# A macaron layer in split fp32: sums spread over the second product's blocks, the passages between its stages rearranged

## The chip, the core and the metric

The kernel runs on one core of a Trainium2 chip. The metric is device time in microseconds of one execution; the kernel before has a median of 1325.62 us over three runs. In the profile PE is TensorE's matmuls, PEld its weight loads, DVE VectorE, ACT ScalarE, POOL GpSimd and SP the engine whose queue issues nearly all the transfers.

## The reference

One layer, 512 tokens of width 1024, all in float32: a feed-forward half step, a token mixer with two branches (a chunked matrix LSTM and an attention with forgetting), and a second feed-forward half step, each with an RMS norm whose gain and shift come from a conditioning vector c.

```python
def swiglu(u, w_in, w_out):
    a, b = jnp.split(u @ w_in, 2, axis=-1)
    return (jax.nn.silu(a) * b) @ w_out

mod = jax.nn.silu(c) @ w_ada + b_ada
sh1, sc1, g1, sh2, sc2, g2, sh3, sc3, g3 = ...
u = rms_norm(x, ffn1_norm_g) * (1 + sc1) + sh1
x = x + 0.5 * g1 * swiglu(u, ffn1_w_in, ffn1_w_out)
u = rms_norm(x, mix_norm_g) * (1 + sc2) + sh2
z = u @ w_mix + b_mix
...
x = x + g2 * (merged @ w_out)
u = rms_norm(x, ffn2_norm_g) * (1 + sc3) + sh3
x = x + 0.5 * g3 * swiglu(u, ffn2_w_in, ffn2_w_out)
```

The hidden width is 2816 (22 blocks of 128), w_mix has some 8200 columns.

## The kernel before

**Split products.** Each float32 product is made of three matmuls on a rounded high half and the rest: hi x hi, lo x hi, hi x lo (mm3, lines 127 to 129; in the passage after FFN1 lines 1397 to 1400). A weight block of 128 x 1024 numbers is loaded into one of three buffers (`raw`, line 92, the loads are issued by SP in order), ScalarE rounds it to the high half (wh, line 102), VectorE subtracts for the low half (wl, line 104); wh and wl have four buffers each. A load may start when the wl that used its buffer three loads earlier is done.

**Activations.** Tokens lie on partitions for x (tiles x[tb][half], four token blocks by two halves of 512 columns) and on the free axis for u = norm(x), which is the transposed xn times G plus sh: ScalarE writes the rounded uh, a second operation the unrounded uf, a third ul = uf - uh. A norm works on two token blocks at once, "half 0" and "half 1", 256 columns of u each: squares on ScalarE as each x tile is finished (x_sq, line 229), a chain of nine small VectorE operations (lines 146 to 154 and 247), four xn, 16 transposes on TensorE (line 295), eight uh, uf and ul.

**Output product of a feed-forward (pair_out, line 515).** The hidden blocks are paired, 11 pairs (NP), and the 512 tokens too, after a Strassen-like scheme: a first product gives sums P1, U2, U4 (two tiles each), the second one works on eight banks X, W, Z, Y, each for two token blocks. Pair i needs a block c of w_out and a block d of precomputed sums of weights (`ws`, in DRAM). i = 0 to 7 run pair by pair; the last three (tail) are closed bank by bank, their d blocks loaded ahead (`early`, we). P1, U2 and U4 are scaled by 0.5 g (line 597) and added to x (line 600) at i = 6 and 7 in the program; where no order is pinned, a scheduler places them. x itself is loaded at i = 3 to 6 into tiles that the first product has used.

**Passages.** After FFN1, `end` closes the banks in a written order (keep_in_program_order, `pin`), adds Z and Y to the first half of the tokens, makes the norm of half 0 while X and W close, and runs the first four column blocks m = 0 to 3 of w_mix on half 0, then on half 1. GpSimd makes every second ul of half 0. After the mixer, token_gemm (half 1 of w_out's columns) makes the last x tiles; norm_half is called for half 0 ahead of the last token block's matmuls and for half 1 behind it, with ul of odd k on GpSimd (line 267) and uf on VectorE (line 266); ffn_in_halves then does the first two hidden blocks of FFN2 by halves. Rows of w_ada for the conditioning vector are worked off in between (acc, line 325).

Of the kernel before, what the change touches and what calls it, by code (L numbers as in the profile page):

```python
# [11 lines left out]
F32 = mybir.dt.float32  # L12
# [8 lines left out]
P = 128  # L21
# [26 lines left out]
class Layer:  # L48
# [209 lines left out]
    def u_from(self, ps, k, c0, w, G, sh, pool):  # L258

        nc = self.nc  # L260
        uf = self.tmp(pool, "uf")
        nc.scalar.activation(self.uh[k][:, c0:c0 + w], ps, AF.Identity, scale=G, bias=sh)
        if self.uf_act:
            nc.scalar.activation(uf[:, :w], ps, AF.Identity, scale=G, bias=sh)
        else:
            nc.vector.tensor_scalar(uf[:, :w], ps, G, sh, op0=MUL, op1=ADD)
        (nc.gpsimd if k % 2 else nc.vector).tensor_tensor(  # L267
            self.ul[k][:, c0:c0 + w], uf[:, :w], self.uh[k][:, c0:c0 + w], op=SUB)

# [12 lines left out]
    def norm_half(self, hf, pool, G, sh):  # L282

        xn = self.xnorm(hf, pool)
        self.norm_u(hf, self.norm_turn(hf, xn), pool, G, sh)

# [11 lines left out]

    def norm_u(self, hf, b, pool, G, sh):
        for k in range(NK):  # L300
            self.u_from(b[k // 2][:, k % 2 * 256:(k % 2 + 1) * 256], k, hf * 256, 256, G[:, k:k + 1], sh[:, k:k + 1], pool)
# [109 lines left out]

    def ffn_in_halves(self, w_in, nj, hp, tp):

        wa = [self.w_stat(w_in, j * P) for j in range(nj)]
        wb = [self.w_stat(w_in, FF + j * P) for j in range(nj)]
        pp = [(self.gbank(), self.gbank()) for _ in range(nj)]
        for h in range(2):
            for j in range(nj):
                c0, c1 = h * 256, (h + 1) * 256
                self.gemm_stat(pp[j][0], wa[j], c0, c1)  # L420
                self.gemm_stat(pp[j][1], wb[j], c0, c1)
                self.pair_h(self.pair_s(pp[j][0], c0, c1, tp), pp[j][1], j, c0, c1, hp, tp)


# [102 lines left out]
    def pair_out(self, w, v, hp, tp, x_src, end=None):  # L527
# [52 lines left out]
        banks = {"Z": Z, "Y": Y, "X": X, "W": W}  # L580
        def prepare(i, d=None):
            c = two(both(2 * i + 1))
            d = d or two(self.ws[i][:, 1:3, :])
# [4 lines left out]
        step = lambda n, tb, i, o: mm(banks[n], tb, *o[n], i == 0, i == NP - 1)  # L588
# [19 lines left out]
        tail, ds = 3, []  # L608
        for i in range(NP - tail):
# [27 lines left out]

        for n in "XZYW":
            for tb in range(2):
                ps = close(n, tb)  # L640
# [9 lines left out]
    def token_gemm(self, lhs, nk, w, half, done, tail=2, extra=None, last=None):  # L650
# [18 lines left out]
        for tb in range(NT):  # L669
            if last and tb == NT - 1:  # L670
                last()
# [4 lines left out]
    def residual(self, factor, v, half, tp, final=False):  # L676
# [3 lines left out]
        def done(tb, half, ps):  # L680
            s = slice(half * 512, (half + 1) * 512)
            t = self.tmp(tp, "rs")
            nc.vector.scalar_tensor_tensor(t, ps, factor, g, op0=MUL, op1=MUL)
            x = self.x[tb][half]
            nc.vector.tensor_tensor(x, x, t, op=ADD)
            if not final:
                self.x_sq(tb, half, t)
            else:
                nc.sync.dma_start(self.out[0, tb * P:(tb + 1) * P, s], x)
# [899 lines left out]
```

## Time and profile before

| | |
|---|---|
| median of three runs | 1325.62 us (1324.99 to 1326.6) |
| profiled execution | 1324.8 us, its span 1323.0 us, granted clock 0.999 |
| busy | PE 1304.9, PEld 1091.7, DVE 958.1, ACT 624.2, POOL 43.7 us |
| chain that ended last | PE 89%, DVE 4%, DMA 3%, ACT 2%, issue 1% |
| FFN1's second product, after which the first passage ends it | about 313 to 376 us of the span |
| second passage | about 955 to 985 us |
| last matmul ends, span ends | 1318.2, 1323.0 us |

A row of the timeline gives start, duration, engine, line of the kernel, operation, output<-inputs, shape, how many of them, and in brackets the idle time before it with what ended it. A row of the windows gives length, then busy time of PE, PEld, DVE, ACT and POOL, PE's granted clock, the share of DMA and GB/s. A row of the waits gives who waited for whom, microseconds in total, times, longest.

### The profile page before, as it was taken

Reading aid. Unit: us, or ns where it says so; the run is one execution under the profiler, and the core shown is the slowest. Engines: PE = TensorE matmul, PEld = TensorE weight load, DVE = VectorE, ACT = ScalarE, POOL = GpSimd, SP = SyncE. Lnnn points to the kernel's source line nnn. Section 1 sums busy time; section 2 is a strip of 40 time slices with the busy share of each in tenths; the row PEclk is TensorE's granted clock in tenths of the full one; section 3 lists DMA queues with packets and bytes.
Section 4 is the critical chain, followed back from the end, with each engine's and each line's share of the span. In section 5 each row is a group of like instructions: output and inputs, shape, how many; then the busy total and the mean of one; then the engine's idle time right before and its main releaser. Section 6 shows DMA issues by size and latency. Waiting matters only on the chain.

```text
span 1323.0 us, 17767 instructions
## 1 busy us (share of the span) xinstructions
PE 1304.9 (99%) x6332; PEld 1091.7 (83%) x6332; DVE 958.1 (72%) x1740; ACT 624.2 (47%) x1038; POOL 43.7 (3%) x65
## 2 busy tenths in 40 slices
PE   7999999999999999999999999999999999999998
PEld 6788888888799888888888788878888888888886
DVE  6877777477788687887877778777577656635777
ACT  5633233355476555566566666334262223223742
POOL 1000000000010101000000000003010000000000
PEclk9999999999999999999999999999999999999999
DMA  9999978465845434533243536777439777624574
GB/s 289 272 327 306 309 251 298 133 195 170 293 118 145 120 104 133 151 104 117 83 120 88 159 98 205 225 245 227 162 97 332 273 233 276 208 96 142 169 260 153
DMA packets 204344, 254.18 MB, mean 192 GB/s; under 512 B 14992, under 2 KB 146480, under 8 KB 204256
## 3 DMA queue, kind: packets, MB, share of 16 engines
q1 hardware_dynamic: 203872, 252.98, 60.0%
q8 instruction: 50, 0.82, 0.3%
q14 instruction: 38, 0.31, 0.1%
q0 software_dynamic: 320, 0.06, 0.0%
q10 hardware_dynamic: 64, 0.02, 0.0%
HBM read 217.28 MB, written 35.72 MB: 191 GB/s over the span
## 4 chain that ended last, share of the span: by engine, by line
PE 89%; DVE 4%; DMA 3%; ACT 2%; issue 1%; SPq 0%; POOL 0%; DVEq 0%; ACTq 0%; POOLq 0%
PE g L129 23%; PE g L127 23%; PE g L128 23%; PE t L128 4%; PE t L129 4%; PE t L127 4%; PE g L825 2%; PE t L1208 1%; PE t L1178 1%; DVE wl L104 1%; DMA x<-x_d 1%; PE t L1149 1%; PE t L825 1%; DMA raw<-in_ffn_w_out_dram 1%; PE t L1150 1%
## 5 line engine op out<-in xcount | busy, mean ns | idle before, releaser
L102 ACT ACTIVATE wh<-raw 128x1024 fp32r<-128x1024 f32 (+2 forms) x250 | 254.2, 1019 | 380.6 <-DMA raw<-in_ffn_w_in_dram 106.4
L104 DVE TENSOR_TENSOR wl<-raw,wh 128x1024 fp32r<-128x1024 f32 (+2 forms) x250 | 293.0, 1174 | 179.3 <-ACT wh L102 155.5
L128 PE MATMUL g<-ul,wh 128*128 128x512 f32 (+1 forms) x912 | 348.1, 383 | 1.1 <-POOL ul L267 1.1
L127 PE MATMUL g<-uh,wh 128*128 128x512 f32 (+1 forms) x912 | 348.7, 384 | 0.0
L129 PE MATMUL g<-uh,wl 128*128 128x512 f32 (+1 forms) x912 | 348.3, 382 | 0.0
L128 PEld LDWEIGHTS g<-ul,wh 128*128 128x128 f32 x912 | 171.3, 188 | 34.5 <-POOL ul L267 1.9
L129 PEld LDWEIGHTS g<-uh,wl 128*128 128x128 f32 x912 | 171.5, 188 | 33.6
L127 PEld LDWEIGHTS g<-uh,wh 128*128 128x128 f32 x912 | 171.0, 188 | 32.5 <-issue 0.6
L325 DVE SCALAR_TENSOR_TENSOR acc<-raw,ccol,acc 128x512 f32<-128x512 f32 (+1 forms) x70 | 66.8, 975 | 43.6 <-DMA raw<-in_w_ada_dram 43.5
L127 PE MATMUL g<-wh,uh 128*128 128x512 f32 (+1 forms) x256 | 97.4, 381 | 0.0
L129 PE MATMUL g<-wh,ul 128*128 128x512 f32 (+1 forms) x256 | 96.6, 378 | 0.0
L128 PE MATMUL g<-wl,uh 128*128 128x512 f32 (+1 forms) x256 | 96.4, 377 | 0.0
L128 PE MATMUL t<-wl,A 128*128 128x512 f32 x176 | 69.0, 392 | 1.7 <-DVE wl L104 1.7
L127 PE MATMUL t<-wh,A 128*128 128x512 f32 x176 | 68.6, 390 | 0.0
L129 PEld LDWEIGHTS g<-wh,ul 128*128 128x128 f32 x256 | 48.1, 188 | 9.0
L127 PEld LDWEIGHTS g<-wh,uh 128*128 128x128 f32 x256 | 48.2, 188 | 8.7 <-DVE tk L1046 0.5
L128 PEld LDWEIGHTS g<-wl,uh 128*128 128x128 f32 x256 | 48.2, 188 | 8.3
L129 PE MATMUL g<-yh,wl 128*128 128x512 f32 x128 | 50.1, 392 | 0.3 <-DVE wl L104 0.3
L127 PE MATMUL g<-yh,wh 128*128 128x512 f32 x128 | 49.8, 389 | 0.0
L128 PE MATMUL g<-yl,wh 128*128 128x512 f32 x128 | 49.8, 389 | 0.0
L455 ACT ACTIVATE A<-E 128x768 fp32r<-128x768 f32 x22 | 18.6, 846 | 57.0 <-DVE E L454 51.1
L1160 ACT ACTIVATE S<-S,mn 128x128 f32<-128x128 f32 (+1 forms) x64 | 35.6, 558 | 16.0 <-DVE mn L1152 9.9
(343 smaller groups left out, 2185.2 us busy)
## 6 DMA issues: line engine op xcount, KB each, us to landing
raw<-in_ffn_w_in_dram SPq DMA_DIRECT2D x82, 512.0 KB, 5.1
raw<-in_w_ada_dram SPq DMA_DIRECT2D x56, 512.0 KB, 5.5
raw<-in_w_mix_dram SPq DMA_DIRECT2D x46, 512.0 KB, 4.5
sa<-in_ffn_w_out_dram SPq DMA_DIRECT2D x22, 512.0 KB, 5.9
sb<-in_ffn_w_out_dram SPq DMA_DIRECT2D x44, 256.0 KB, 5.9
ws<-sa SPq DMA_DIRECT2D x22, 512.0 KB, 3.9
ws<-sb SPq DMA_DIRECT2D x44, 256.0 KB, 4.2
raw<-ws SPq DMA_DIRECT2D x44, 256.0 KB, 3.5
```

The lines of the kernel that those rows point to most:

```text
L102: nc.scalar.activation(hi, src, AF.Copy)
L104: self.last_lo = nc.vector.tensor_tensor(lo, src, hi, op=SUB)
L127: pin(mm(ps, lh, rh, start=start, stop=False))
L128: pin(mm(ps, lh, rl, start=False, stop=False))
L129: self.last_mm = pin(mm(ps, ll, rh, start=False, stop=stop))
L325: nc.vector.scalar_tensor_tensor(a, r[:, s], c, a, op0=MUL, op1=ADD)
L455: nc.scalar.activation(A1[:, 0:3, :], E[:, 0:3, :], AF.Copy)
L825: pin(nc.tensor.matmul(acc_ps[b], (wl if p == 1 else wh)[:, b % 2, s], self.ul[k] if p == 2 else self.uh[k], start=k == 0 and p == 0, stop ...
L1149: nc.tensor.matmul(ps[:, :w], q[:, s], k[:, :w], start=True, stop=False)
L1150: nc.tensor.matmul(ps[:, :w], q[:, s], kl[:, :w], start=False, stop=True)
L1160: nc.scalar.activation(S[:, ws], S[:, ws], AF.Exp, scale=-1.0, bias=m, accum_out=sm[:, qb:qb + 1])
L1178: tr = lambda b, c, qb, kb: nc.tensor.transpose(b[:, c:c + P], S[:, P_OFF[qb] + kb * P:P_OFF[qb] + (kb + 1) * P], self.ident)
```

## The change

**pair_out, both feed-forwards.** The d block of odd i up to 7 is loaded into a fourth buffer of its own (`two_x`, a tile with the tag "xn", the space of a tile that the first half of pair_out has used) and not into the ring. P1, U2 and U4 are scaled in place at i = 0, 1 and 2, and added to x at i = 4 to 7, one token block each time. Their number stays: six scalings, eight sums.

**End of FFN2.** Bank W[1]'s accumulation is closed after i = 7 and its sum added early; the last three pairs of it go into two banks of 256 columns, each scaled, added and stored by itself.

**First passage.** ScalarE copies the X banks to SBUF (`keep`); `other` scales the copy for one half, `both` adds the W bank to the copy, and one scaling of this sum serves where two were. The high halves of m = 2, 3 are placed behind the copies.

**Second passage.** token_gemm's second half, the norm and FFN2's first blocks are written out in one pinned order (`passage`): the transposes of half 0 come after the first three matmuls of the last token block, uf is all ScalarE's and ul all VectorE's, the first four weight blocks of FFN2's w_in run on half 0 (m = 0, 1, then 2, the transposes of half 1, then 3) and then on half 1; the pairs' silu and product come behind, 512 columns at a time.

```diff
+        def two_x(src):
+            t = tp.tile(sh, F32, name=self.nm("raw"), tag="xn", bufs=1)
+            nc.sync.dma_start(t, src)
+            return self.split(t, sh)
...
-            d = d or two(self.ws[i][:, 1:3, :])
+            d = d or (two_x if i % 2 else two)(self.ws[i][:, 1:3, :])
...
-            if i in (6, 7):
-                tb = i - 6
-                add(P1[tb], 0, (tb,))
-                add(U2[tb], 0, (tb + 2,))
-                add(U4[tb], 1, (tb, tb + 2))
+            for src, half in ((P1, 0), (U2, 0), (U4, 1))[i:i + 1]:
+                for tb in range(2):
+                    scaled(src[tb], half, src[tb])
+            if i >= 4:
+                tb = i - 4
+                onto(tb, 0, (P1, U2)[tb // 2][tb % 2])
+                onto(tb, 1, U4[tb % 2])
...
+        add(W[1], 0, (3,))
         for n in "XZYW":
             for tb in range(2):
+                if n == "W" and tb:
+                    for c in (slice(0, 256), slice(256, 512)):
+                        ps, x, r = self.gbank((P, 256)), self.x[3][0][:, c], slice(P, 2 * P)
...
+                        t = self.tmp(tp, "rs")[:, :256]
+                        nc.vector.scalar_tensor_tensor(t, ps, 0.5, g[0][:, c], op0=MUL, op1=MUL)
+                        V(x, x, t, op=ADD)
+                        nc.sync.dma_start(self.out[0, 3 * P:4 * P, c], x)
+                    continue
...
                     X = [close("X", tb) for tb in range(2)]
                     W = [close("W", 0)]
+                    xs = [keep(tb, 0) for tb in range(2)]
+                    pin(nc.scalar.activation(xs[0], X[0], AF.Copy))
+                    hi2()
                     xn = self.xnorm(0, tp)
                     b = self.norm_turn(0, xn)
                     W.append(close("W", 1))
-                    tx = {}
-                    for tb in range(2):
-                        for h in (1, 0):
...
-                            tx[tb, h] = scaled(X[tb], h, t)
+                    pin(nc.scalar.activation(xs[1], X[1], AF.Copy))
+                    hi3()
+                    x1 = {}
+                    def other(tb):
+                        x1[tb] = scaled(xs[tb], 1, keep(tb, 1))
+                    def both(tb):
+                        pin(V(xs[tb], W[tb], xs[tb], op=ADD))
+                    other(0)
+                    both(0)
+                    scaled(xs[0], 0, xs[0])
+                    other(1)
...
-                    w0 = scaled(W[0], 0)
+                    both(1)
                     lo1(4, NK)
```

The second passage's core:

```diff
+        xn = self.xnorm(0, bp)
+        step(3, 1, wcs[0], (0,))
+        b = self.norm_turn(0, xn)
+        step(3, 1, wcs[0], (1,))
+        step(3, 2, wcs[1])
+        step(3, 3, wcs[2])
...
+        first(0, (0, 1))
+        hi3()
+        lo3()
+        first(0, (2,))
+        b = self.norm_turn(1, xn)
+        first(0, (3,))
+        for k in range(NK):
+            part(1, b, k, True)
+        first(1, (0, 1))
+        first(1, (2,))
+        first(1, (3,))
```

**Where it moves instructions.** SP's queue at the start of FFN1's second product, before: c and d blocks in turn (raw from in_ffn1_w_out_dram is a c, raw from ws a d; ws_741 is d0, ws_742 d1, and so on).

```order
L92 DMA raw_2792<-in_ffn_w_out_dram 128x1024 [waits DMAHW6_49,DMAHW5_49,DVE_49]
L92 DMA raw_2798<-ws_741 128x1024 [waits DMAHW1_49,DMAHW0_49,DVE_49]
L92 DMA raw_2828<-in_ffn_w_out_dram 128x1024 [waits DMAHW4_49,DMAHW7_49,DMAHW3_49,DVE_49]
L92 DMA raw_2834<-ws_742 128x1024 [waits DMAHW5_49,DVE_49]
L92 DMA raw_2864<-in_ffn_w_out_dram 128x1024 [waits DMAHW6_49,DVE_49,Activation_49]
L92 DMA raw_2870<-ws_743 128x1024 [waits DMAHW2_49,DMAHW7_49,DVE_49,Activation_49]
L92 DMA raw_2900<-in_ffn_w_out_dram 128x1024 [waits DMAHW0_49,DVE_49]
L92 DMA raw_2906<-ws_744 128x1024 [waits DMAHW1_49,DVE_49]
```

The same place after:

```order
L92 DMA raw_2792<-in_ffn_w_out_dram 128x1024 [waits DMAHW6_49,DMAHW5_49,DVE_49]
L92 DMA raw_2798<-ws_741 128x1024 [waits DMAHW1_49,DMAHW0_49,DVE_49]
L92 DMA raw_2830<-in_ffn_w_out_dram 128x1024 [waits DMAHW4_49,DMAHW7_49,DMAHW3_49,DVE_49]
L92 DMA raw_2868<-in_ffn_w_out_dram 128x1024 [waits DMAHW5_49,DVE_49]
L92 DMA raw_2874<-ws_743 128x1024 [waits DMAHW6_49,DVE_49]
L507 DMA raw_2836<-ws_742 128x1024 [waits DMAHW2_49,DVE_49]
L92 DMA raw_2906<-in_ffn_w_out_dram 128x1024 [waits DMAHW7_49,DVE_49]
L507 DMA raw_2912<-ws_744 128x1024 [waits DMAHW2_49,DVE_49]
```

d1 and d3 are now issued at line 507 into their own buffer and stand one place later: c2 and d2 go ahead of d1, c4 no longer waits for d3's slot.

VectorE in the first passage, behind the xn of half 0, before (g_2780 and g_2781 are the X banks, g_2782 and g_2783 the W banks, wl of L1336 the low halves of m = 1 to 3).

```order
L597 SCALAR_TENSOR_TENSOR rs_3315<-g_2780,gb_2790 128x512 [waits PE_49]
L597 SCALAR_TENSOR_TENSOR rs_3317<-g_2780,gb_2788 128x512
L597 SCALAR_TENSOR_TENSOR rs_3319<-g_2781,gb_2790 128x512 [waits PE_49]
L597 SCALAR_TENSOR_TENSOR rs_3321<-g_2781,gb_2788 128x512
L280 TENSOR_TENSOR ul_3278<-uf_3323,uh_3270 128x256 [waits Activation_49]
L597 SCALAR_TENSOR_TENSOR rs_3331<-g_2782,gb_2788 128x512 [waits PE_49]
L1336 TENSOR_TENSOR wl_3184<-raw_3181,wh_3183 128x512
L280 TENSOR_TENSOR ul_3280<-uf_3334,uh_3272 128x256 [waits Activation_49]
L1336 TENSOR_TENSOR wl_3216<-raw_3213,wh_3215 128x512 [waits DMAHW5_49]
L597 SCALAR_TENSOR_TENSOR rs_3343<-g_2783,gb_2788 128x512 [waits PE_49,Pool_49]
L1336 TENSOR_TENSOR wl_3221<-raw_3218,wh_3220 128x512 [waits DMAHW6_49]
```

The same place after (L1437 is `both`, L1409 the low halves, L268 is ul).

```order
L566 SCALAR_TENSOR_TENSOR rs_3313<-rs_3242,gb_2790 128x512 [waits Activation_49]
L1437 TENSOR_TENSOR rs_3242<-g_2782,rs_3242 128x512 [waits DVE_49,PE_49]
L566 SCALAR_TENSOR_TENSOR rs_3242<-rs_3242,gb_2788 128x512 [waits DVE_49]
L566 SCALAR_TENSOR_TENSOR rs_3317<-rs_3243,gb_2790 128x512 [waits Activation_49]
L268 TENSOR_TENSOR ul_3274<-uf_3319,uh_3266 128x256 [waits Activation_49]
L1437 TENSOR_TENSOR rs_3243<-g_2783,rs_3243 128x512 [waits DVE_49,PE_49]
L1409 TENSOR_TENSOR wl_3178<-raw_3175,wh_3177 128x512
L268 TENSOR_TENSOR ul_3276<-uf_3329,uh_3268 128x256 [waits Activation_49]
L1409 TENSOR_TENSOR wl_3210<-raw_3207,wh_3209 128x512 [waits DMAHW5_49]
L1409 TENSOR_TENSOR wl_3214<-raw_3211,wh_3213 128x512 [waits DMAHW6_49]
L268 TENSOR_TENSOR ul_3278<-uf_3339,uh_3270 128x256 [waits Activation_49]
```

The scalings of X[1] and W[1] are gone from the front, and two sums that wait for a W bank stand ahead of the low halves and of the ul behind them.

VectorE in the second passage before, from the xn of half 1 on (t_9356 and on are the transposes' banks, L266 makes uf, L267 ul, L448 belongs to FFN2's first hidden block).

```order
L253 TENSOR_SCALAR xn_9348<-x_8927,rq_9336 128x512 [waits DVE_49]
L253 TENSOR_SCALAR xn_9352<-x_8929,rq_9336 128x512
L266 TENSOR_SCALAR uf_9376<-t_9356,G_9099,sh_9098 128x256 [waits Activation_49,Pool_49]
L267 TENSOR_TENSOR ul_9252<-uf_9376,uh_9244 128x256 [waits DVE_49]
L266 TENSOR_SCALAR uf_9380<-t_9356,G_9099,sh_9098 128x256 [waits Activation_49]
L266 TENSOR_SCALAR uf_9384<-t_9357,G_9099,sh_9098 128x256 [waits PE_49,Pool_49]
L448 TENSOR_TENSOR Ra_9550<-g_9447,sl_9548 128x256 [waits PE_49]
L267 TENSOR_TENSOR ul_9254<-uf_9384,uh_9246 128x256 [waits DVE_49]
L266 TENSOR_SCALAR uf_9388<-t_9357,G_9099,sh_9098 128x256 [waits Activation_49]
L266 TENSOR_SCALAR uf_9392<-t_9358,G_9099,sh_9098 128x256
```

The same place after, behind the xn of half 1 (L268 is ul; wl_9339 is FFN2's fourth block, wl_9661 and wl_9708 are the two behind it).

```order
L690 TENSOR_TENSOR wl_9339<-raw_9336,wh_9338 128x1024 [waits DMAHW0_49,Activation_49]
L104 TENSOR_TENSOR wl_9661<-raw_9658,wh_9660 128x1024 [waits DMAHW1_49,Activation_49]
L104 TENSOR_TENSOR wl_9708<-raw_9705,wh_9707 128x1024 [waits DMAHW3_49,Activation_49]
L268 TENSOR_TENSOR ul_9269<-uf_9500,uh_9261 128x256 [waits Activation_49]
L268 TENSOR_TENSOR ul_9270<-uf_9504,uh_9262 128x256 [waits Activation_49]
L268 TENSOR_TENSOR ul_9271<-uf_9508,uh_9263 128x256 [waits Activation_49]
L268 TENSOR_TENSOR ul_9272<-uf_9512,uh_9264 128x256 [waits Activation_49]
L302 TENSOR_SCALAR acc_9757<-raw_9758,ccol 128x1024 [waits DMAHW6_49,DMAHW0_49]
L268 TENSOR_TENSOR ul_9273<-uf_9516,uh_9265 128x256 [waits Activation_49]
L268 TENSOR_TENSOR ul_9274<-uf_9520,uh_9266 128x256 [waits Activation_49]
L268 TENSOR_TENSOR ul_9275<-uf_9524,uh_9267 128x256 [waits Activation_49]
```

Before, the same eight ul alternated between VectorE and GpSimd with uf between them, and the acc of this row of w_ada stood 15 rows behind the last ul of half 1, among the first hidden block's work; now it stands between the fourth and the fifth ul.

More of the change, by code (lines that the diff above doesn't have):

```diff
@@ L587, in prepare @@
             return {"Z": (a(0), b(0)), "Y": (a(3), b(1)), "X": (a(2), b(2)), "W": (a(1), b(3))}
-        step = lambda n, tb, i, o: mm(banks[n], tb, *o[n], i == 0, i == NP - 1)
+        step = lambda n, tb, i, o: mm(banks[n], tb, *o[n], i == 0, i == NP - (1 if end or n != "W" or not tb else 1 + tail))
         if end:
@@ L648, in pair_out, with token_gemm @@
                     store(q, half)
-    def token_gemm(self, lhs, nk, w, half, done, tail=2, extra=None, last=None):
+    def token_gemm(self, lhs, nk, w, half, done, tail=2, extra=None):
         nch = nk // 2
@@ L687, in done @@
                 self.x_sq(tb, half, t)
-            else:
-                nc.sync.dma_start(self.out[0, tb * P:(tb + 1) * P, s], x)
+            return t
         return done
@@ L1344, in end, with keep @@
                     lo1(0, 4)
-                    lo2, lo3 = hi(2), hi(3)
+                    hi2, lo2 = fetch(2)
+                    hi3, lo3 = fetch(3)
+                    def keep(tb, h):
+                        return hp.tile([P, 512], F32, name=self.nm("rs"), tag=f"{('Ra', 'Rb')[h]}{5 + tb}", bufs=1)
                     X = [close("X", tb) for tb in range(2)]
                     W = [close("W", 0)]
+                    xs = [keep(tb, 0) for tb in range(2)]
+                    pin(nc.scalar.activation(xs[0], X[0], AF.Copy))
+                    hi2()
                     xn = self.xnorm(0, tp)
@@ L1368, in end @@
                     lo2(0, 4)
-                    w1 = scaled(W[1], 0)
                     lo3(0, 4)
@@ L1543, in run @@
             x_spill(1)
-            self.ffn_in_halves(A["ffn2_w_in"][0], 2, hp, tp)
+            for j in range(2):
+                self.pair_h(self.pair_s(pp[2 * j], 0, T, tp), pp[2 * j + 1], j, 0, T, hp, tp)
             new = lambda: [tp.tile([P, D], F32, name=self.nm("acc"), tag="xn", bufs=1)]
```

157 lines of the change are left out of this document (101 added, 56 removed).

## The prediction

> **What bounds the kernel now.** I read the profile page first (busy shares, chain), then the table of windows, the list of waits of TensorE, and then the timelines of the stretches that the change touches.
>
> ```profile
> PE 1304.9 (99%) x6332; PEld 1091.7 (83%) x6332; DVE 958.1 (72%) x1740; ACT 624.2 (47%) x1038; POOL 43.7 (3%) x65
> PE 89%; DVE 4%; DMA 3%; ACT 2%; issue 1%; SPq 0%; POOL 0%; DVEq 0%; ACTq 0%; POOLq 0%
> 345.00:360.00 15.00, 14.32 (x62) 11.23 (x61) 10.86 (x10) 7.45 (x8) 0.00 (x0) 1.00 0.83 278
> 360.00:395.00 35.00, 34.52 (x230) 31.38 (x229) 29.40 (x64) 25.04 (x52) 5.44 (x8) 1.00 0.49 134
> 960.00:1000.00 40.00, 38.78 (x273) 35.51 (x273) 31.67 (x63) 21.10 (x36) 5.88 (x8) 1.00 0.43 149
> 1260.00:1300.00 40.00, 38.97 (x171) 31.64 (x170) 29.41 (x32) 17.89 (x17) 0.00 (x0) 1.00 0.84 289
> PE t L128 <- DVE wl L104: 1.7, 3, 0.7
> PE g L128 <- POOL ul L267: 1.1, 3, 0.5
> ```
>
> TensorE is busy for 1304.9 of 1323.0 us, at a granted clock of 1.00 in all four windows, and the change takes no matmul away. So it can only win idle time of TensorE. The four windows hold all of the places it touches but the last stretch, and TensorE's idle time there is 0.68 + 0.48 + 1.22 + 1.03 = 3.4 us; the waits in it are for weights' low halves (wl, VectorE) and for the GpSimd part of ul. A wait costs more than its bracket says, because the matmuls are pipelined: matmuls of 512 columns start every 0.23 us, of 256 columns every 0.12, and a late start counts by the spacing. No part can win more than a few us; about 0.2% (2.65 us) is what a measurement of this kernel can tell from no change.
>
> **FFN1's output product: which load goes where.**
>
> ```profile
> 346.32 0.50 PE L128 MATMUL t<-wl,A 128*128 128x512 f32 x1
> 346.30 0.33 SPq L92 DMA_DIRECT2D raw<-ws  x1
> 348.03 5.35 SPq L92 DMA_DIRECT2D raw<-in_ffn_w_out_dram  x3
> 357.16 1.06 ACT L102 ACTIVATE wh<-raw 128x1024 fp32r<-128x1024 f32 x1 [1.43 <-DMA raw<-in_ffn_w_out_dram]
> 358.25 1.23 DVE L104 TENSOR_TENSOR wl<-raw,wh 128x1024 fp32r<-128x1024 f32 x1 [1.27 <-ACT wh L102]
> 358.49 0.39 PE L127 MATMUL t<-wh,A 128*128 128x512 f32 x1
> 359.54 0.50 PE L128 MATMUL t<-wl,A 128*128 128x512 f32 x1 [0.65 <-DVE wl L104]
> 314.98 0.69 DVE L482 TENSOR_TENSOR Rb<-R,A 128x512 fp32r<-128x512 f32 x1
> 321.35 0.39 PE L127 MATMUL g<-wh,A 128*128 128x512 f32 x1
> raw<-ws SPq DMA_DIRECT2D x1, 512.0 KB, 7.2
> ```
>
> The load of w_out's last block but none is issued as the last of three between 348.03 and 353.4: the ring of three has to give a slot back, and d7 (346.30) holds one. It lands at 357.16, high half 1.06, low half 1.23, and the low half is 0.82 late for the matmul at 359.54 (1.05 from start to start, less 0.23), with another 0.1 in the one behind it. With d1, d3, d5 and d7 in a buffer of their own this load is some 5 us earlier and both this (0.93) and a smaller wait go, the one at 346.32, which shows the same 0.50 for 0.39 and starts 0.19 late, 0.3 with the one behind it: +1.25.
>
> In return d1 now waits for the buffer that R held, whose last reader is the second row of L482. Two scalings of P1 fewer stand ahead of that row and one wl more, which puts its end at about 316.2 and not at 315.7; and d1 stands behind d2 in SP's queue. Issued at 316.25, with the 3.9 us that such loads mostly take here (353.1 to 357.16 above), it lands at 320.2; high half to 321.26, low half 1.23 more, 322.5. Bank X of i = 1 starts at 321.35 with four matmuls that need only the high half, so the low half is due at 321.35 + 4 x 0.23 = 322.25. That is a wait of 0.25 to 0.35; nothing, if it lands in 3.6, and 3.5 if it takes the 7.2 us of the slow row (323.5 + 1.06 for the high half, against 321.35, with low half behind). I take 0.35. Net +0.9 (from -2.3 to +1.25). The spread sums are the same fourteen VectorE operations at other places; cover for them is the time in which VectorE waits for a high half (1.27 in the row above).
>
> **First passage.** VectorE has 15 operations of 512 columns behind the first xn, for 17; two copies of PSUM banks are new on ScalarE, 0.53 each by the first row (1.06 for two), which put its chain of uh and uf (before: from 373.00) about 0.35 later.
>
> ```profile
> 310.37 1.06 ACT L571 ACTIVATE P<-t 128x512 f32<-128x512 f32 x2
> 373.00 0.56 ACT L275 ACTIVATE uh<-t,sh,G 128x256 fp32r<-128x256 f32 x1 [1.25 <-PE t L295]
> 371.03 2.48 DVE L597 SCALAR_TENSOR_TENSOR rs<-g,gb 128x512 f32<-128x512 f32 x4
> 375.02 1.26 POOL L280 TENSOR_TENSOR ul<-uf,uh 128x256 fp32r<-128x256 f32 x1 [367.70 <-ACT uf L277]
> 375.88 0.68 DVE L280 TENSOR_TENSOR ul<-uf,uh 128x256 fp32r<-128x256 f32 x1 [0.20 <-ACT uf L277]
> 378.28 0.41 DVE L280 TENSOR_TENSOR ul<-uf,uh 128x256 fp32r<-128x256 f32 x1
> 375.94 0.39 PE L129 MATMUL g<-we,Ra 128*128 128x512 f32 x1
> 378.08 0.40 PE L1400 MATMUL g<-ul,wh 128*128 128x256 f32 x2
> 387.56 0.88 DVE L253 TENSOR_SCALAR xn<-x,rq 128x512 f32<-128x512 f32 x2
> 388.19 2.16 PE L295 MATMUL t<-ident,xn 128*128 128x128 f32 x16 [0.36 <-DVE xn L253]
> ```
>
> Before, the four scalings at 371.03 need only the X banks, and VectorE runs on. Now the second operation, both(0), needs bank W[0], which closes at about 372.5, and both(1) needs W[1], whose last matmul is the row at 375.94: it can't start before 376.35. It stands ahead of lo1(4..), ul2, lo2 and lo3. So VectorE does other(0), waits till 372.6, does both(0), scaled, other(1) (0.60 each, from 2.48 for four) and ul0 until 374.8, then waits again: 376.35 + 0.65 + 0.60 puts ul2 at 377.6 instead of 375.88. From there each operation with two SBUF sources meets GpSimd: the ul at 375.88 took 0.68 beside GpSimd's, the one at 378.28 0.41 alone. So ul2 is ready at 378.0 with no hindrance, at about 378.65 with one GpSimd operation in the way. The matmul pair of ul2 and ul3 is the row at 378.08: a stall of 0 to 0.6, and a second like it at lo3, due 1.9 later with lo2 and lo3 between. The x sums then end about 0.9 later than before (386.1 for 385.2), and xn, at 387.56 before, comes at about 388.6; the transposes, which already wait for xn at 388.19, move by as much. The two early stalls are inside that 1.05, not beside it. I take -1.05: from -1.5 (GpSimd meets every one) to +0.5 (it meets none; two operations of 0.60 fewer then end the x sums early, and the wait of xn, 0.36 by its bracket, goes).
>
> The Trainium skill's page "SBUF — State Buffer", section "Who interferes with whom", says that VectorE and GpSimd hold one shared port pair in turn, for a whole instruction each. By that rule the ul at 375.88 waited for GpSimd's end at 376.28, which the trace fits (0.40 + 0.28), and my -1.05 stands; without it the result would be near the +0.5 end.
>
> **Second passage.**
>
> ```profile
> 960.28 0.39 PE L127 MATMUL g<-wh,mh 128*128 128x512 f32 x1
> 960.79 2.15 PE L295 MATMUL t<-ident,xn 128*128 128x128 f32 x16
> 966.68 0.28 PE L127 MATMUL g<-uh,wh 128*128 128x256 f32 x1
> 981.95 0.28 PE L129 MATMUL g<-uh,wl 128*128 128x256 f32 x1
> 982.76 0.39 PE L128 MATMUL g<-ul,wh 128*128 128x256 f32 x1 [0.53 <-POOL ul L267]
> raw<-in_w_ada_dram SPq DMA_DIRECT2D x56, 512.0 KB, 5.5
> DMA to landing us min/median/max: 2.6/4.7/8.2
> ```
>
> By spacing, TensorE loses 2.6 us in five gaps, the first around the transposes at 960.79 (0.5: they start 0.28 late and run 0.2 over), the last at 982.76 (0.81 - 0.12, and 0.1 behind it); the three between wait for GpSimd's ul or a wl. All go: the transposes come three matmuls (0.68) later, ul is VectorE's alone, and the uf that VectorE made are ScalarE's. About 0.3 stays for the second transposes.
>
> New is one operation in VectorE's order: acc of the next w_ada row stands between the fourth and the fifth ul of half 1 and waits for a 512 KB load, whose issue waits for a slot that the second wl behind xn gives back. xn comes at about 974.4 at its end (uf and the wl's are out of its way), two wl make it 977.2. With 5.5 us the load lands at 982.7, acc takes 0.75 (512 columns of one source take 0.44 in the xn row of the first passage, less overlap), ul 0.42: ready at 983.85. TensorE starts half 0 at 966.15, needs 96 x 0.1195 = 11.5 for its four blocks, 1.95 for transposes, and comes to the fifth ul 27 matmuls of half 1 later, about 982.6. A stall of 1.25; 0 with a load of 4.2 us or less, 3.9 with the 8.2 that is the longest of all loads of raw. Net 2.6 - 0.3 - 1.25 = +1.0 (from -1.6 to +2.3).
>
> **FFN2's output product and the end.**
>
> ```profile
> 1279.09 0.50 PE L128 MATMUL t<-wl,A 128*128 128x512 f32 x1 [0.39 <-DVE wl L104]
> 1290.90 0.50 PE L128 MATMUL t<-wl,A 128*128 128x512 f32 x1 [0.63 <-DVE wl L104]
> 1274.76 0.69 DVE L600 TENSOR_TENSOR x<-x,rs 128x512 f32<-128x512 f32 x1 [1.09 <-DMA x<-x_d]
> 1318.20 0.69 DVE L597 SCALAR_TENSOR_TENSOR rs<-g,gb 128x512 f32<-128x512 f32 x1 [0.62 <-PE g L129]
> 1318.93 0.69 DVE L600 TENSOR_TENSOR x<-x,rs 128x512 f32<-128x512 f32 x1
> ```
>
> The same two waits as in FFN1 stand here: 0.39 and 0.63 in brackets, with the 0.17 and 0.1 that the wait at 359.54 had on top 1.57. The d1 load is no problem, its buffer is free long before. I take +1.4, since a sum that waits for x (1.09 in the row at 1274.76) can still hold up one wl: +0.4 to +1.57. At the end scaling and sum take 0.69 each of 512 columns; of 256 about 0.41, so 0.56 goes, 18 matmuls of 0.12 for 9 of 0.23 cost some 0.1, and the last matmul's own drain is 0.1 shorter: +0.55. The store stays behind it.
>
> **Sum.** 0.9 - 1.05 + 1.0 + 1.4 + 0.55 = 2.8 us less. The profiled execution took 1324.8 (span 1323.0 and 1.8 around it), which gives 1322.0; it lies 0.82 below the median of the three runs, and carried to that median the forecast is 1325.62 - 2.8 = **1322.8**.
>
> **Rivals.**
> - First passage unhindered: GpSimd's operations fall beside those of VectorE with a PSUM source. Then +0.6 for -1.05: about 1321.2. For: one ul at 378.28 took 0.41 in the middle of it. Against: 0.68 at 375.88.
> - Waits only move: in the second passage the load of w_ada takes its 8.2, or the new order brings other gaps, and in FFN2 one of the two stays: the forecast less 2.0, 1324.8. So the change doesn't do what it says there.
> - FFN1's d1 is late, 7.2 us from issue: a stall of 3.5 for 0.35, about 1326.0. It decides from a landing of over 4 us, and eats the whole gain near 7.
> - Slower: the spread x sums. They stand between the low halves of i = 4 to 7 in both products, eight groups, and each waits for its x load; in the row at 1274.76 such a wait was 1.09, and the wl behind it came 0.56 late at 1279.09. With 0.56 to 0.8 for each of eight, 5.4 us, and the 2.3 of the FFNs' gain gone with it in part (1.0), the time is about 1329. It decides when an x load, issued during one i, lands after the next i's first low half is due, that is in over one i, 24 x 0.23 = 5.4 us; against it, the sums of before already stood between low halves there, and only two waits came of it.
>
> **Chances.** Forecast 0.40, unhindered 0.20, moved 0.15, d1 late 0.13, spread sums 0.12. The limit of faster (1322.97) lies just above my number, so the forecast's own spread of about 1 us is split 0.25 faster, 0.15 same. Faster: 0.25 + 0.20 = 0.45; same: 0.15 + 0.15 + 0.13 = 0.43; slower 0.12. The range takes in all but the last and the outer part of unhindered: 1320.3 to 1326.4.
>
> **What would show it.** Right: no wait of t on wl near 358 and 1290, no wait on GpSimd behind 960, xn of half 1 in the first passage about 1 us later, a wait of up to 1.3 us on ul near 982, and 0.5 us less between last matmul and last store. Wrong: waits on wl at i = 4 to 7 behind sums of x (the slower rival), a wait at X of i = 1 near 321 of over 1 us, or a transposing block of the first passage that no longer waits.

## The result, and the profile after

| | before | after |
|---|---|---|
| median | 1325.93 us (1324.41 to 1326.69, 6 runs) | 1321.19 us (1320.37 to 1322.25, 6 runs) |
| profiled execution, its span | 1324.8, 1323.0 us | 1321.06, 1319.3 us |

The ratio is 0.9967, 95% interval 0.9956 to 0.9977: 4.4 us less, with 3.0 to 5.8 in the interval. The forecast was 1322.8, 2.8 less. A second set, beside the experiments (11 runs of the changed kernel, median 1322.46), gave 0.9977 (0.9968 to 0.9986), 3.0 us less. The two intervals share 3.0 to 4.2 us.

First the busy shares of the page, then the same four windows as before (length, busy time of PE, PEld, DVE, ACT and POOL, PE's clock, share of DMA, GB/s), then the waits of TensorE at the places of the change.

```profile
PE 1302.9 (99%) x6341; PEld 1091.7 (83%) x6341; DVE 953.4 (72%) x1734; ACT 630.6 (48%) x1056; POOL 36.8 (3%) x57
345.00:360.00 15.00, 15.00 (x68) 12.43 (x67) 10.91 (x10) 7.64 (x8) 0.00 (x0) 1.00 0.76 263
360.00:395.00 35.00, 34.19 (x227) 30.93 (x226) 28.31 (x62) 25.97 (x54) 4.52 (x8) 1.00 0.51 140
960.00:1000.00 40.00, 39.59 (x281) 36.92 (x280) 24.33 (x52) 28.03 (x50) 0.00 (x0) 1.00 0.45 150
1260.00:1300.00 40.00, 40.00 (x178) 33.14 (x177) 31.70 (x34) 18.58 (x18) 0.00 (x0) 1.00 0.76 263
PE g L128 <- DVE ul L268: 0.4, 1, 0.4
PE t L278 <- DVE xn L253: 0.4, 1, 0.4
PE g L1484 <- DVE ul L268: 0.4, 1, 0.4
PE g L129 <- DVE wl L104: 0.2, 1, 0.2
```

TensorE's idle time in the four windows was 0.68, 0.48, 1.22 and 1.03 us and is 0, 0.81, 0.41 and 0: both output products and the second passage have lost their waits, the first passage has gained one. The waits of t on wl and of g on GpSimd's ul are gone from the list.

For a finer balance I matched TensorE's instructions of two traces by number (6332 before; the nine more of after all come at the end) and took the difference of their starts. The scheduler orders some matmuls of one size differently, so it is the n-th start against the n-th start. The difference moves only where one kernel waits and the other doesn't:

| stretch (before's time) | after minus before, change over the stretch | forecast |
|---|---|---|
| start to 312 | +0.43 (first load, not part of the change) | |
| FFN1's product: 312 to 330, 330 to 345, 345 to 376 | +0.51, -0.08, -1.29: together -0.86 | -0.9 |
| first passage, 376 to 395 | +0.60 | +1.05 |
| 395 to 880; 880 to 900 | +0.37; -0.37 | |
| second passage, 955 to 1000 | -1.80 | -1.0 |
| FFN2's product, 1250 to 1300 | -1.37 | -1.4 |
| from there to the end of the span | -0.70 | -0.55 |

The sum is -3.7, the difference of the two spans. Every place has the sign that the forecast gave it.

The places where after still waits, in TensorE's, VectorE's and GpSimd's timelines:

```profile
322.02 1.07 PE L127 MATMUL g<-wh,A 128*128 128x512 f32 x4
323.06 0.50 PE L128 MATMUL g<-wl,A 128*128 128x512 f32 x1
375.93 0.69 DVE L1437 TENSOR_TENSOR rs<-g,rs 128x512 f32<-128x512 f32 x1 [1.33 <-PE g L129]
377.14 0.96 DVE L268 TENSOR_TENSOR ul<-uf,uh 128x256 fp32r<-128x256 f32 x1
376.95 0.87 POOL L268 TENSOR_TENSOR ul<-uf,uh 128x256 fp32r<-128x256 f32 x1 [1.08 <-ACT uf L265]
378.16 0.51 PE L1484 MATMUL g<-ul,wh 128*128 128x256 f32 x2 [0.35 <-DVE ul L268]
388.41 0.85 PE L278 MATMUL t<-ident,xn 128*128 128x128 f32 x4 [0.39 <-DVE xn L253]
977.33 0.33 SPq L92 DMA_DIRECT2D raw<-in_w_ada_dram  x1
982.16 0.75 DVE L302 TENSOR_SCALAR acc<-raw,ccol 128x1024 f32<-128x1024 f32 x1 [1.26 <-DMA raw<-in_w_ada_dram]
983.30 0.39 PE L128 MATMUL g<-ul,wh 128*128 128x256 f32 x1 [0.41 <-DVE ul L268]
```

At 322 the low half of d1 is late behind four matmuls that need only its high half (0.25 by the starts). At 375.93 the sum with bank W[1] has kept VectorE waiting for 1.33; ul2 follows a low half later, and takes 0.96 beside GpSimd's. At 982.16 acc has waited 1.26 for its load and hands 0.67 of it on.

### The profile page after: what moved, and what is told of

Same layout as the page of the kernel before. It is cut to its first block, busy times and chain, and to the rows that moved or that the text cites. A ratio compares the mean times of both kernels' runs of the same rounds, so it can differ in the third digit from the quotient of the medians.

```text
span 1319.3 us, 17786 instructions
## 1 busy us (share of the span) xinstructions
PE 1302.9 (99%) x6341; PEld 1091.7 (83%) x6341; DVE 953.4 (72%) x1734; ACT 630.6 (48%) x1056; POOL 36.8 (3%) x57
## 4 chain that ended last, share of the span: by engine, by line
PE 91%; DVE 4%; ACT 2%; DMA 1%; issue 1%; POOL 0%; ACTq 0%; POOLq 0%; DVEq 0%
PE g L129 23%; PE g L127 23%; PE g L128 23%; PE t L127 4%; PE t L129 4%; PE t L128 4%; PE g L897 2%; PE t L1280 1%; PE t L1250 1%; PE t L1221 1%; PE t L897 1%; PE t L1222 1%; DVE wl L104 1%; DVE fq L1200 0%; POOL rowsA L171 0%
## 5 line engine op out<-in xcount | busy, mean ns | idle before, releaser
L102 ACT ACTIVATE wh<-raw 128x1024 fp32r<-128x1024 f32 (+2 forms) x246 | 249.2, 1017 | 381.3 <-PE g L128 116.3
L104 DVE TENSOR_TENSOR wl<-raw,wh 128x1024 fp32r<-128x1024 f32 (+2 forms) x246 | 287.0, 1169 | 162.3 <-ACT wh L102 140.3
L127 PE MATMUL g<-uh,wh 128*128 128x512 f32 (+1 forms) x880 | 340.9, 387 | 0.0
L128 PE MATMUL g<-ul,wh 128*128 128x512 f32 (+1 forms) x880 | 339.5, 386 | 0.4 <-DVE ul L268 0.4
L129 PE MATMUL g<-uh,wl 128*128 128x512 f32 (+1 forms) x880 | 339.6, 386 | 0.0
L129 PEld LDWEIGHTS g<-uh,wl 128*128 128x128 f32 x880 | 165.3, 188 | 33.5
L128 PEld LDWEIGHTS g<-ul,wh 128*128 128x128 f32 x880 | 165.4, 188 | 33.2 <-DVE ul L268 0.6
L127 PEld LDWEIGHTS g<-uh,wh 128*128 128x128 f32 x880 | 165.4, 188 | 32.6 <-issue 0.6
```

What stands on the lines that cost most here:

```text
L102: nc.scalar.activation(hi, src, AF.Copy)
L104: self.last_lo = nc.vector.tensor_tensor(lo, src, hi, op=SUB)
L127: pin(mm(ps, lh, rh, start=start, stop=False))
L128: pin(mm(ps, lh, rl, start=False, stop=False))
L129: self.last_mm = pin(mm(ps, ll, rh, start=False, stop=stop))
```

## The experiments

Each of the first nine is one profiled run; what it changes is read from its trace, place by place, by the same matching, against the changed kernel. The times of single runs are given for the record and don't rank the versions: the kernel before, beside them, took 1329.26 us in the first four, 1324.8 in the next four and 1325.79 (median of 15) in the last.

**The odd d blocks back in the ring of three.**

```diff
-            d = d or (two_x if i % 2 else two)(self.ws[i][:, 1:3, :])
+            d = d or two(self.ws[i][:, 1:3, :])
```

> The changed kernel with one thing put back: the odd d blocks are loaded into the ring of three again (two for two_x), the sums stay spread. Theory A, the waits at the end of both second products went because these loads left the ring: waits of t on wl of 0.6 to 1.3 us come back in both products (together +2.3 us by TensorE's starts), and the 0.5 us that the changed kernel lost near 314 and 323 goes at least by its half at 323. Net about +1.8 us against the changed kernel. Rival B, the spread sums took them away: no wait of t on wl comes back, the time falls by 0.2 to 0.5 us.

```profile
346.74 0.50 PE L128 MATMUL t<-wl,A 128*128 128x512 f32 x1 [0.38 <-DVE wl L104]
360.19 0.51 PE L128 MATMUL t<-wl,A 128*128 128x512 f32 x1 [0.76 <-DVE wl L104]
348.44 5.53 SPq L92 DMA_DIRECT2D raw<-in_ffn_w_out_dram  x3
358.91 1.23 DVE L104 TENSOR_TENSOR wl<-raw,wh 128x1024 fp32r<-128x1024 f32 x1 [1.35 <-ACT wh L102]
```

In FFN1 both waits are back, and the last of the three loads is held back as in the kernel before (5.53 us for three issues): +1.87 over 345 to 365, and -0.26 where d1 no longer waits. That is 0.58 more than the change had won there (1.29), so with the ring this order of VectorE's work is the worse one; what in it costs that no run separates. In FFN2 nothing comes back: 0.00 from 1250 to 1300. So theory A holds in FFN1 and falls in FFN2. (1325.68 us in this run; 3.1 us of its surplus arose near 880, of which below, and 0.36 in the untouched first passage.)

**The sums late again, the buffer kept.**

```diff
-            for src, half in ((P1, 0), (U2, 0), (U4, 1))[i:i + 1]:
...
+            if i in (6, 7):
+                tb = i - 6
+                add(P1[tb], 0, (tb,))
+                add(U2[tb], 0, (tb + 2,))
+                add(U4[tb], 1, (tb, tb + 2))
```

> The changed kernel with the sums of P1, U2 and U4 at i = 6 and 7 as before; the odd d blocks keep their own buffer. Theory A (the buffer did it): no wait of t on wl in either product's second half, total within 0.5 us of the changed kernel; at i = 1 the low half of d1 is no longer behind four scalings. Rival B (the spread did it): waits of 0.6 to 1.3 us near 358 and 1290 come back, +2 us.

No wait came back near 358 or 1290 (0.00 and -0.21). Against the expectation, 312 to 330 got 0.79 longer: the low half of d1 kept TensorE waiting for 0.8 (bracket), since with another order of the scheduler the low half is the second matmul of its bank and not the fifth. 1320.75 us.

Together the two show different causes at the two places. In FFN1 the wait at 359.54 was a load held back by the ring. In FFN2 it took both the ring and the late sums; taking away either is enough. VectorE in the kernel before, ahead of the low half that is late at 1290.90:

```profile
1285.95 0.69 DVE L600 TENSOR_TENSOR x<-x,rs 128x512 f32<-128x512 f32 x1 [0.41 <-DMA x<-x_d]
1286.56 1.22 DVE L546 TENSOR_TENSOR we<-we,we 128x1024 fp32r<-128x1024 f32 x1
...
1289.02 0.69 DVE L600 TENSOR_TENSOR x<-x,rs 128x512 f32<-128x512 f32 x1
1289.63 1.22 DVE L104 TENSOR_TENSOR wl<-raw,wh 128x1024 fp32r<-128x1024 f32 x1
```

It works without a break from 1285.95 on, after a wait for x, into the late low half; it isn't the high half that is late there.

**The first passage as before, all else changed.** (The functions put, scaled and onto as in the kernel before; no keep, both and other.)

> The changed kernel with the first passage as before (X scaled twice from PSUM, no copies), everything else changed. Theory A, the new first passage costs 0.6 us because a sum that waits for bank W[1] stands ahead of a low half and ul2 on VectorE: the wait of 0.4 on ul near 377 goes, xn of half 1 comes 0.6 us earlier against TensorE, the time from the first matmul of w_mix to the end of the passage is 0.6 us shorter. Rival B, two VectorE operations fewer are a gain: the passage gets 0.3 to 1 us longer.

From 375.7 to 395 of after's time it gains 0.52 (no wait on ul2: -0.61, then +0.09): theory A. Its span is 0.37 longer than the changed kernel's all the same (1321.42 us), because at 880 to 900 TensorE waited 1.62 more.

**The second passage as before, all else changed.** (token_gemm with `last`, norm_half, ffn_in_halves; ul of odd k on GpSimd.)

> The changed kernel with the second passage as before (GpSimd makes the ul of odd k, VectorE the uf, the first hidden blocks by halves with their silu between), everything else changed. Theory A: the stretch between TensorE's 955 and 1000 gets 1.8 us longer, with three waits of g on GpSimd's ul (1.1 us together by their brackets) and none on acc's ul. Rival B, the gain there is only that acc of w_ada was moved or that the silu pairs are whole: fewer than two waits on GpSimd, under 1 us.

```profile
969.53 0.39 PE L128 MATMUL g<-ul,wh 128*128 128x256 f32 x1 [0.34 <-POOL ul L267]
972.28 0.39 PE L128 MATMUL g<-ul,wh 128*128 128x256 f32 x1 [0.21 <-POOL ul L267]
983.92 0.38 PE L128 MATMUL g<-ul,wh 128*128 128x256 f32 x1 [0.53 <-POOL ul L267]
```

The three waits on GpSimd are back and the stretch from 955 to 999 is 1.78 longer (1323.87 us): theory A. By the starts the three are 1.86 of it; the rest, the transposes and a wl, is about what the changed kernel loses to acc (0.66). What the other parts of the rearrangement would bring alone no run shows.

**acc behind the last ul of the second passage.**

```diff
         for k in range(NK):
-            part(1, b, k, True)
+            self.last_ul = self.u_part(1, b, k, bp, G, sh, True, nc.vector)()
```

> The changed kernel with acc of the w_ada row placed behind the last ul of half 1 in the second passage, not between the fourth and the fifth. Theory A, the wait near 982 is acc's wait for its load, handed on to ul: the stretch of TensorE from 965 to 999 gets 0.67 us shorter and the wait of g on ul there goes. Rival B, ul there waits for ScalarE's uf (one pair each 0.91 us) in any case: the wait shrinks by less than 0.3.

```profile
981.47 0.42 DVE L268 TENSOR_TENSOR ul<-uf,uh 128x256 fp32r<-128x256 f32 x1 [0.48 <-ACT uf L265]
984.54 0.75 DVE L302 TENSOR_SCALAR acc<-raw,ccol 128x1024 f32<-128x1024 f32 x1
```

The wait on ul is gone, 965 to 990 is 0.66 shorter (1320.53 us). Theory A.

**The sum with W[1] behind ul2 and ul3.**

```diff
-                    both(1)
                     lo1(4, NK)
                     part(2, 3)
                     u[2]()
                     u[3]()
+                    both(1)
                     lo2(0, 4)
```

> The changed kernel with the sum of bank W[1] (both(1)) placed behind ul2 and ul3 in the first passage, where the scaling of W[1] stood before. Theory A, the wait of TensorE on ul2 comes from that sum's wait for the bank: the 0.5 us near 377.5 goes, and since VectorE no longer idles there xn of half 1 comes up to 0.5 us earlier against TensorE; stretch 375.7 to 390 shorter by 0.5 to 1.0 us, against that of before still 0 to 0.1 longer. Rival B, GpSimd's port use makes ul2 late: the wait stays at 0.3 or more.

```profile
374.75 0.68 DVE L1409 TENSOR_TENSOR wl<-raw,wh 128x512 fp32r<-128x512 f32 x1
375.94 0.42 DVE L268 TENSOR_TENSOR ul<-uf,uh 128x256 fp32r<-128x256 f32 x1 [0.51 <-ACT uf L265]
376.29 0.69 DVE L1437 TENSOR_TENSOR rs<-g,rs 128x512 f32<-128x512 f32 x1
387.82 1.40 PE L278 MATMUL t<-ident,xn 128*128 128x128 f32 x9
```

VectorE now works where it waited for 1.33, the waits on ul2 and on xn are both gone, 375.7 to 389.9 is 0.94 shorter: theory A, and 0.3 less than the passage took before. (1322.14 us: again 1.57 lost at 880 to 900, and 0.77 at 335, where one low half of FFN1 was late.)

**No ul on GpSimd in the first passage.**

```diff
-   ... self.u_part(0, b, k, tp, G, sh, True, nc.gpsimd if k % 2 else nc.vector)
+   ... self.u_part(0, b, k, tp, G, sh, True, nc.vector)
```

> The changed kernel with all eight ul of the first passage's half 0 on VectorE, none on GpSimd. Theory A (the sum that waits for W[1] holds ul2 up): the wait near 377.5 stays or grows to 0.5 to 0.9, because the ul of odd k join the queue behind it; xn of half 1 moves by -0.3 to +0.5 us, four more ul of 0.34 against the 0.5 each that VectorE's operations lose beside GpSimd. Rival B (the shared port is what costs): the wait near 377.5 goes below 0.2 and xn comes at least 0.5 us earlier.

```profile
375.67 0.69 DVE L1437 TENSOR_TENSOR rs<-g,rs 128x512 f32<-128x512 f32 x1 [0.65 <-PE g L129]
376.88 0.75 DVE L268 TENSOR_TENSOR ul<-uf,uh 128x256 fp32r<-128x256 f32 x2
385.39 0.73 DVE L146 TENSOR_SCALAR rq<-v 128x2 int32<-128x2 int32 x1
385.57 0.53 POOL L962 MEMSET ggm<- 64x512 f32 x1
387.34 0.88 DVE L253 TENSOR_SCALAR xn<-x,rq 128x512 f32<-128x512 f32 x2
```

Rival B's part: two ul take 0.75 here, one took 0.96 beside GpSimd, and the wait on ul2 shrank from 0.51 to 0.07 (0.22 appeared at lo3). The last x sum ends 0.64 earlier against TensorE, but xn only 0.17, and the passage gained only 0.18 (1322.3 us): one small operation of the norm (L146), 0.27 in the changed kernel and 0.17 before, took 0.73 here and ended 0.02 after a GpSimd memset that ran beside it. That memset as the cause is read from the rows and not tested. Theory A, that ul2 stays late whatever GpSimd does, falls, though moving the sum removed the wait too. So ul2 was late by the sum's wait and by GpSimd's operation together; without either one it is in time. The Trainium skill's page "SBUF — State Buffer", section "Who interferes with whom", says that a VectorE instruction with two SBUF inputs contends with a GpSimd instruction that reads SBUF, for a port pair that is locked for one of them. In the changed kernel the ul of 377.14 ends 0.28 after GpSimd's at 377.82, which agrees.

**d1 alone back in the ring.**

```diff
-            d = d or (two_x if i % 2 else two)(self.ws[i][:, 1:3, :])
+            d = d or (two_x if i % 2 and i > 1 else two)(self.ws[i][:, 1:3, :])
```

> The changed kernel with only the load of d1 (i = 1) back in the ring of three in both products; d3, d5 and d7 keep their own buffer. Theory A, the 0.5 us that the changed kernel loses in FFN1 near 314 to 323 is d1's wait for a buffer that R's readers hold until 316.7: at least the 0.25 at 323 goes, and no wait of t on wl comes back near 358 or 1290: 0.2 to 0.5 us shorter between 312 and 330. Rival B, the loss comes from the low half of d0 being scheduled elsewhere or from the scalings ahead of it: less than 0.1 us changes.

312 to 330 is 0.26 shorter, 345 to 365 unchanged: theory A for half of the 0.51. The 0.22 at 314 stays; it belongs to d0's low half, which is due earlier in the new order; that reading has no run of its own. 1321.08 us.

**The end of FFN2 in one piece.** (W[1] closed like W[0].)

> The changed kernel with W[1]'s end whole again: nine matmuls of 512 columns, one scaling, one sum, one store. Theory A: the time from TensorE's last matmul to the end of the span grows from 4.0 to 4.55 to 4.8 us (0.56 of VectorE, the rest in the drain of the last matmul and a store twice as big), TensorE ends 0.1 earlier, net +0.5 to +0.7. Rival B, the two stores of 256 columns cost what the halves win: the end is within 0.2 us.

From the last of the unchanged matmuls to the end of the span it is 0.70 longer: 0.20 - 0.31 = -0.11 for TensorE, 0.81 behind it. Theory A, at its upper end (1322.08 us).

**The three moves together, beside the changed kernel.**

> The changed kernel with three things moved, by the runs before: acc behind the last ul of the second passage (-0.67 us there), the sum of bank W[1] behind ul2 and ul3 in the first (-0.9), d1 back in the ring (-0.3). If the three places are independent, as theory A has them: about 1.8 us under the changed kernel on the same chip, no wait of g on ul at 377 and 982. Rival B, they share a limit later (the x chain, the load queue): under 1 us.

> The changed kernel as it is, beside the version above on one chip. The ratio to the kernel before should be 0.9967 within 0.001; by the places of the trace, -4.1 of 1325.9, 0.9969.

The version with the three moves took 1320.42 us (5 runs), ratio to the kernel before 0.9960 (0.9946 to 0.9974); the changed kernel 1322.46 (11 runs), 0.9977 (0.9968 to 0.9986), at the edge of what was expected of it, the kernel before 1325.79. All three gains are in its trace: -0.27, -1.02 and -0.66, together 1.95, as independent as expected. But its profiled span is only 0.65 below the changed kernel's, because near 880 it loses 1.6 of what it was ahead. The medians differ by 2.0, about the sum of the places, but the intervals overlap: of the versions that I ran several times it has the lowest median, and by how much is not settled.

**What takes the time back.** TensorE in the changed kernel, then in the version with the three moves (with an earlier matmul in each), then in the latter the block's load, its high half, and VectorE, and last the changed kernel's high half:

```profile
881.06 0.39 PE L128 MATMUL g<-yl,wh 128*128 128x512 f32 x1
881.69 0.50 PE L129 MATMUL g<-yh,wl 128*128 128x512 f32 x1 [0.24 <-DVE wl L104]
880.04 0.39 PE L128 MATMUL g<-yl,wh 128*128 128x512 f32 x1
881.71 0.50 PE L129 MATMUL g<-yh,wl 128*128 128x512 f32 x1 [1.28 <-DVE wl L104]
870.51 6.36 DMA raw<-in_w_branch_b_dram
876.89 1.06 ACT L102 ACTIVATE wh<-raw 128x1024 fp32r<-128x1024 f32 x1 [2.90 <-DMA raw<-in_w_branch_b_dram]
879.11 1.41 DVE L304 SCALAR_TENSOR_TENSOR acc<-raw,ccol,acc 128x512 f32<-128x512 f32 x2
880.43 1.22 DVE L104 TENSOR_TENSOR wl<-raw,wh 128x1024 fp32r<-128x1024 f32 x1
876.87 1.06 ACT L102 ACTIVATE wh<-raw 128x1024 fp32r<-128x1024 f32 x1 [1.32 <-DMA raw<-in_w_branch_b_dram]
```

The second kernel comes to this matmul 1.0 us earlier and starts it at the same time. Its load was issued at 870.5 and landed 6.4 us later, at 876.9; in the changed kernel it was issued at 871.7 and landed at 876.8. In all thirteen traces up to here this low half ends 4.8 us after the landing and the matmul starts 0.05 to 0.06 later, so it is this landing, with the fixed order of ScalarE and VectorE behind it, that sets when TensorE gets past. From issue to landing it took 5.0 to 6.8 us. In eight of the thirteen, those of before and after among them, TensorE passes 900 us within 0.2 of the changed kernel, although they reach 880 us up to 1.6 apart. The others passed it 0.4 to 4.7 later; in four of these five the load landed 0.7 to 4.6 later too, and the kernel with the ring, which reached 880 us 3.0 late, lost another 1.7 there. So what comes early is held here, and what comes late is not made up. I tried to move it:

```diff
+                w = self.w_stat(A["w_branch_b"][0], (m + 1) * P) if m == 0 else None
                 step()
```

> The version with the three things moved, and in the untouched branch stage the second w_branch_b block fetched ahead of a row of w_ada (its load ahead on SP's queue, its low half ahead of two acc on VectorE). In all traces so far TensorE waits near 880 us for that low half, 0.2 to 1.4 us, the longer the earlier it comes; in eight of the twelve it reaches 900 us within 0.3 of the same time. Theory A, this place takes back what is won before it: the wait goes below 0.2, TensorE reaches 900 us 1.4 us earlier than in the version without it, and the time is about 1.4 us lower, 1319.0 beside a kernel before of 1325.8. Rival B, the load queue sets the pace there: the wait only moves to a later block, under 0.4 us.

```profile
874.78 1.06 ACT L102 ACTIVATE wh<-raw 128x1024 fp32r<-128x1024 f32 x1 [5.61 <-DMA raw<-in_w_branch_b_dram]
875.75 4.26 ACT L1349 ACTIVATE yh<-yb 128x512 fp32r<-128x512 f32 x8
PE g L127 <- ACT yh L1349: 1.1, 1, 1.1
PE g L129 <- DVE wl L104: 0.5, 1, 0.5
PE g L127 <- ACT wh L102: 0.2, 1, 0.2
```

Theory A's remedy fell: the old wait shrank (2.0 less by starts), but the block fetched ahead also has its high half ahead of the eight yh on ScalarE, which waits 5.61 us for the load and makes them late (1.1 by the list, 1.9 by starts), and a later block costs 0.7 by the list, 1.3 by starts. From 395 to 900 us it loses 1.2 more than the version without the move. The time was 1322.54 us, ratio 0.9969 (0.9957 to 0.9981), where 1319.0 had been expected. That the landing sets the pace of this place is shown by the traces. Why a load issued earlier lands no earlier stays open, and so does what it would bring to put the low half alone ahead of the two acc.

## Why the prediction was right, and where its steps were off

- **The sum: near, and in part by luck.** The five places came to 4.1 us for 2.8 forecast; the second passage gave 0.8 and the first 0.45 more than forecast. With 0.43 lost at the first load, which is no part of the change, the spans differ by 3.7. The first set's median, 1321.2, is the number of the rival "unhindered", but that rival did not happen: it has the first passage gain 0.6, and it lost 0.60. The second set's 1322.46 is 0.3 from the forecast.
- **FFN1's product, 0.9 forecast, 0.86 measured.** The ring held the late load, and the buffer of its own ended that (the kernel with the ring: +1.87 there). d1 does wait for R's readers: their last row ends at 316.75, d1 is issued at 316.78, two places later in the queue than before (d3 stays where it was), and is 0.25 late in the changed trace, as the 0.25 to 0.35 of the text. It landed 3.9 us after its issue, so the rival of a d1 at 7.2 us did not come (the 3.9 was right, though the row that the text gives for it, 353.1 to 357.16, is 4.1). Not foreseen: 0.22 more at 314. The 0.79 of the kernel with late sums shows how much this place can cost.
- **First passage, -1.05 forecast, -0.60 measured.** The mechanism stands: the sum waits for W[1], ul2 comes 0.5 late, and xn late behind it. The size was off in the last step: xn came about 0.6 later relative to TensorE and not 1.05. Behind the first xn, VectorE saves two operations (1.2 us) and waits 0.76 more; beside GpSimd three of its operations are stretched, as many as before, and they lose only 0.27 more (1.64 for 1.37: two ul of 0.96 and 0.95, and one wl in the first row below, 1.83 for a pair that takes 1.28 at 378.03). The second stall, at lo3, is not in this trace, but 0.42 to 0.44 by starts in six of the other seven with this passage unchanged, where the wait on xn shrinks by about as much in all but one: the early stalls are inside the wait on xn, as the text had it.

```profile
380.71 1.83 DVE L1409 TENSOR_TENSOR wl<-raw,wh 128x512 fp32r<-128x512 f32 x2
380.59 0.80 POOL L268 TENSOR_TENSOR ul<-uf,uh 128x256 fp32r<-128x256 f32 x1 [0.69 <-DMA raw<-in_w_mix_dram]
```

- **Second passage, +1.0 forecast, +1.80 measured.** The five gaps went, and the one new wait is acc's, at the place given. The load was issued at 977.33 against 977.2 forecast, but landed after 4.8 us and not 5.5: a wait of 0.67 for 1.25. By the text's own terms TensorE comes to the fifth ul at 982.8 and not 982.6, which makes the stall 1.05; this slip is 0.2 of the difference. And the gaps around the transposes closed to 0.2.
- **FFN2's product, +1.4 forecast, +1.37 measured, by a wrong reason.** The text took the two waits for those of FFN1. The ring alone isn't their cause: with the ring back and the sums spread they stay away. That the buffer came together with the spread sums, either of which is enough, made the number right. The two waits were worth 0.67 and 0.91 by starts, and 0.22 was lost at 1257, as at 314 in FFN1.
- **The end, +0.55 forecast, +0.70 measured.** VectorE's part was as worked out (0.54); with the store of half the size the span ends 0.28 sooner after the last sum (3.09 us, against 3.37 before and with the end in one piece), which the text had at nothing.
- **The slower rival** (spread sums in front of low halves) did not come. VectorE does wait for x there, as these rows of the changed kernel show, but TensorE does not wait once in that window:

```profile
1269.02 0.69 DVE L569 TENSOR_TENSOR x<-x,U 128x512 f32<-128x512 f32 x1 [0.45 <-DMA x<-x_d]
1286.39 0.69 DVE L569 TENSOR_TENSOR x<-x,U 128x512 f32<-128x512 f32 x1 [1.29 <-DMA x<-x_d]
```

- **What no step had:** that time won before 880 us counts only as far as the load near 877 lands earlier. TensorE passes 900 us 0.17 later than before: +0.43 from the first load, -0.86 and +0.60 from FFN1 and the first passage, +0.37 from 395 to 880 (nearly all near 415, where a small product of the mixer is late, in the kernel with the first passage as before too) and -0.37 from 880 to 900. So the 3.7 us between the two spans are those of the second passage, FFN2 and the end (1.80 + 1.37 + 0.70, less 0.17). Since the forecast for the first two places was nearly nothing together (0.9 - 1.05), the sum hardly felt it.

## What to carry to other kernels

Where an engine is busy for 99%, list its gaps by the spacing of its starts, not by the waits alone, and work out each edit against its own gap: the five places of this change, 0.6 to 1.8 us each, came out with the right sign this way, one of them by a wrong reason. An instruction that waits for a late bank or a slow load must not stand ahead of short work that is due at once (both(1), acc): moving each behind it was worth 0.94 and 0.66 us. And ask for each gain whether a later stage, paced by something else, takes it back.

## What the runs showed that I had not expected

A 512 KB load issued 1.2 us earlier landed at the same time (870.5 and 871.7, both near 876.9), in a stretch where no step of the change lies. Two waits that look alike in the list, of t on wl in the two products, had different causes, and one of them needed two causes at once.
